# Rotary halves and residual rows added by accumulating DMAs, and new copy durations in a planner

## The chip, the core and the metric

The kernel runs on one core of a Trainium2 chip. A core has TensorE (PE) for matmuls and transposes, VectorE (DVE), ScalarE (ACT) and GpSimd (POOL) for elementwise work, SyncE (SP) whose queue issues the DMAs, 128 partitions of SBUF, and eight PSUM banks of 128 x 512 float32. The metric is the device time of one execution in microseconds (us). Lower is better.

## What is computed

A decoder trunk of two layers in float32 on 1024 tokens of width 1024:

```
x <- x + RMSNorm( W_out [ retention | dilated attention | gated MLP ] ( RMSNorm(x) ) )
x <- x + RMSNorm( W_down ( silu(W_gate h) * W_up h ) ),  h = RMSNorm(x)
```

All mixers read one input projection. Queries and keys of the 6 retention heads and the 6 attention heads (64 wide) get a rotary embedding: `t * cos + rot * sin`, where `rot = concat(-t[32:], t[:32])` swaps the two halves of a head and negates one. The two things the change is about are this sum and the residual sum `x + RMSNorm(f) * g`.

## The kernel before

**Precision by splitting.** Each float32 operand of a large matmul is split into a high part (a rounded copy, tiles `wh`, `hT`, `ph`, `ga`, `wb`) and a low part (source minus high part, `wl`, `pl`), and a product is three matmuls. The copy runs on ACT or DVE, the subtraction on DVE. Banks of 512 columns are evacuated by ACT or DVE.

**Order.** Every helper (`tt`, `stt`, `copy`, `act`, `dma`, `mm`) only records an operation in a `Program`, with its possible engines and a cost in ns for each. Two planners use these costs. While operations are recorded (`Program.add`), a clock per engine estimates when data is ready; generators such as `att_pair`, `ret_pair` and `post_norm` go on when their inputs are ready by that clock, and this sets the order of recording. Then `Program.order` simulates the engines with all operations: whichever is ready with the earliest due time goes next, PE's due times follow the recorded order, and an operation with two engines goes where it would end first. The outcome is the fixed order of instructions on every engine; semaphores make an engine wait where data comes later than planned. For a DMA on SP both planners add 650 ns, the bytes at 360 per ns behind the DMAs before it, and 1000 ns to the issue's cost.

**A rotary half.** A projection of 128 features (two heads) by 1024 tokens is made in two halves of 512 tokens, each a bank `fb` (`feat`). `rope_evac` copies the bank to `z`, has four DMAs of 64 KB copy `z` to `sw` with groups of 32 partitions swapped, and computes `r = z * cos`, `sw = sw * sin`, `r = r + sw`. The sine table carries the sign (`K_SIGN`). There are 24 halves per layer: 12 in the attention part, 12 in the retention part. In attention `r` is read by `att_pair` (copies `ks` of the key) and `att_unit` (copies `qd` of the query), which run as four lanes of softmax work between the projections; in retention by `ret_pair`, whose transposes and score matmuls read `r` directly.

**A residual tile.** `post_norm` is called for each of 8 token tiles after the output projection and after the feed-forward part, in both layers (32 calls). It loads the old row block `xt` (512 KB) early, computes the norm of `f` (ACT square, POOL power in `rms`), multiplies `f` by the gain row, computes `xt = f * ss + xt`, stores `xt`, and, except in the last of the four stages, makes the next norm (`prenorm`, into `nj`) and transposes it on PE (`to_hT`, banks `tb`) into `hT` for the next projection.

POOL runs only the powers of the norms (`ss`, `gn`) and a few memsets; all DMAs are issued on SP.

Of the kernel before, what the change touches and what calls it, by code (L numbers as in the profile page):

```python
# [15 lines left out]
ALU = mybir.AluOpType  # L16
AX = mybir.AxisListType

P = 128
S = 1024  # L20
D = 1024
NT = S // P
NK = D // P
DEPTH = 2
HD = 64
# [11 lines left out]
K_ID, K_TRIL, K_DEC, K_XI, K_ZETA, K_GAM, K_FREQ, K_SIGN, K_END = (  # L37
    0, 128, 256, 1024, 1408, 1414, 1417, 1449, 1577)
# [36 lines left out]
def _constants():  # L75
    c = np.zeros((P, K_END), np.float32)
    i = np.arange(P)
    c[:, K_ID:K_ID + P] = np.eye(P)
    c[:, K_TRIL:K_TRIL + P] = i[:, None] >= i[None, :]
    lg = np.log(1.0 - 2.0 ** (-5.0 - np.arange(6)))  # L80
    diff = (i[None, :] - i[:, None]).astype(np.float64)
    for h in range(6):
        c[:, K_DEC + h * P:K_DEC + (h + 1) * P] = np.where(
            diff >= 0, np.exp(-lg[h] * (i[:, None] + 1.0)) * HD ** -0.5, 0.0)
        c[:, K_ZETA + h] = np.exp(lg[h] * (P - 1.0 - i)) * HD ** -0.5
    for p in range(3):
        for e in range(2):
            rows = slice(e * HD, (e + 1) * HD)
            c[rows, K_XI + p * P:K_XI + (p + 1) * P] = np.exp(lg[2 * p + e] * (i + 1.0))[None]
            c[rows, K_GAM + p] = np.exp(lg[2 * p + e] * P)  # L90
    c[:, K_FREQ:K_FREQ + 32] = (10000.0 ** (-np.arange(0, HD, 2) / HD))[None]
    c[:, K_SIGN:K_SIGN + P] = np.where(i % HD < HD // 2, -1.0, 1.0)[None]

    dist = (NT - 1) * P + i[:, None] - np.arange(S)[None, :]
    count = np.zeros(dist.shape)
    for window, dil in ((128, 1), (512, 4), (2048, 16)):
        count += (dist >= 0) & (dist <= window) & (dist % dil == 0)
    with np.errstate(divide="ignore"):
        mask = np.where(count > 0, HD ** 0.5 * np.log(count), NEG)
    return c, mask.astype(np.float32)  # L100
# [109 lines left out]
class Program:  # L210
# [17 lines left out]
    def add(self, alts, outs, ins, nbytes=0, func=None, **args):  # L228

        op = Op()  # L230
        eng = min(alts, key=lambda e: self.t[e] + alts[e][0])
        cost = alts[eng][0]
        op.alts, op.eng, op.cost, op.args, op.nbytes, op.func = alts, eng, cost, args, nbytes, func
        op.name = outs[0].root.name if outs else ""
        deps = set()
        for r in ins:
            t, (a, b, lo, hi) = r.root, r.box
            for o, w in t.writes:
                if t.psum or (w[0] < b and a < w[1] and w[2] < hi and lo < w[3]):
                    deps.add(o)  # L240
            if t.psum:
                deps.update(o for o, _ in t.reads)
        for r in outs:
            t, (a, b, lo, hi) = r.root, r.box
            hit = False
            for o, w in t.writes:
                if t.psum or (w[0] < b and a < w[1] and w[2] < hi and lo < w[3]):
                    deps.add(o)
                    hit = True
            for o, w in t.reads:  # L250
                if t.psum or (w[0] < b and a < w[1] and w[2] < hi and lo < w[3]):
                    deps.add(o)
            if not hit:
                deps.update(t.before)
        for r in outs:
            t, (a, b, lo, hi) = r.root, r.box
            for x in (t.writes, t.reads):
                x[:] = [(o, w) for o, w in x if t.psum and False or not (
                    a <= w[0] and w[1] <= b and lo <= w[2] and w[3] <= hi) or (t.psum and o.eng != eng)]
            t.writes.append((op, (a, b, lo, hi)))  # L260
        for r in ins:
            r.root.reads.append((op, r.box))
        deps.discard(op)
        op.deps = deps
        self.list.append(op)

        t = self.t[eng]
        for r in ins:
            for k in self.keys(r):
                if r.root.by.get(k) != eng:  # L270
                    t = max(t, r.root.done.get(k, r.root.since))
        for r in outs:
            for k in self.keys(r):
                if r.root.last.get(k) != eng:
                    t = max(t, r.root.used.get(k, r.root.since))
        end = t + cost
        self.t[eng] = end
        if eng == "sp":
            self.t["bw"] = max(self.t["bw"], end + 650) + nbytes / 360
            end = self.t["bw"] + 1000  # L280
        lag = LAT.get((eng, "pe"), 0.0)
        for r in ins:
            for k in self.keys(r):
                if end + lag > r.root.used.get(k, 0.0):
                    r.root.used[k], r.root.last[k] = end + lag, eng
        for r in outs:
            for k in self.keys(r):
                r.root.done[k] = r.root.used[k] = end + lag
                r.root.by[k] = r.root.last[k] = eng

    def order(self):
# [10 lines left out]
                d.users.append(o)  # L302
        for o in reversed(ops):
            if o.eng != "pe":
                cost = o.cost + (o.nbytes / 360 + 1650 if o.eng == "sp" else 0.0)
                o.prio = min((u.prio - LAT.get((o.eng, u.eng), 0.0) * SLACK for u in o.users), default=t) - cost * SLACK
        free = dict(pe=0.0, act=0.0, dve=0.0, pool=0.0, sp=0.0)
        bw, table = 0.0, None
# [23 lines left out]
        while len(done) < len(ops):  # L332
# [38 lines left out]
                table = o.func  # L371
            o.start = best
            o.end = free[eng] = best + o.cost
            if eng == "sp":
                bw = max(bw, o.end + 650) + o.nbytes / 360
                o.end = bw + 1000
            done.append(o)
# [97 lines left out]
def _body(ctx, tc, nc, x, positions, g_mix_pre, g_mix_post, w_in, w_s, b_s, w_out,  # L475
# [36 lines left out]
    def dma(out, in_):  # L512
        outs = [out] if isinstance(out, Ref) else []
        ins = [in_] if isinstance(in_, Ref) else []
        n = 4 * math.prod((outs + ins)[0].shape)
        prog.add(dict(sp=(475.0 if n > 66000 else 650.0, nc.sync.dma_start)), outs, ins, n, out=out, in_=in_)

    in_all = (AF.Copy, AF.Identity, AF.Square)

    def act_cost(o, i, n_ptr=0):  # L520
        return 0.833 * o.size + (51 if i.root.psum else 93) + 93 * n_ptr

    def act(o, i, func=AF.Copy, **kw):
        ptrs = [v for k, v in kw.items() if k != "accum_out" and isinstance(v, Ref)]
# [5 lines left out]
    def copy(o, a, only=None):  # L530

        alts = dict(act=(act_cost(o, a), lambda out, in_: nc.scalar.activation(out=out, in_=in_, func=AF.Copy)),  # L532
                    dve=((1.042 if a.root.psum else 0.521) * o.size + 68, nc.vector.tensor_copy))
        if only:
            alts = {only: alts[only]}
        prog.add(alts, [o], [a], out=o, in_=a)

    def tt(o, a, b, op, on=None):

        alts = {}  # L540
        if on != "pool":
            alts["dve"] = (1.042 * o.size + 68,
                           lambda out, in0, in1: nc.vector.tensor_tensor(out=out, in0=in0, in1=in1, op=op))  # L543
        if on != "dve" and op != ALU.max and not (a.root.psum or b.root.psum):
            alts["pool"] = (300 + 165 * o.size if op == ALU.pow else 150 + 2.11 * o.size,
                            lambda out, in0, in1: nc.gpsimd.tensor_tensor(out=out, in0=in0, in1=in1, op=op))  # L546
        prog.add(alts, [o], [a, b], out=o, in0=a, in1=b)
# [432 lines left out]

    def post_norm(t, f, g_post, g_pre, src, dst, raw=False):

        while U.left < 2:
            yield None
        xt = U.alloc(name="x")
        dma(xt[:], src[t * P:(t + 1) * P, :])
        tmp = U.alloc(name="nj")
        cuts = halves if g_pre is None and t == NT - 1 else whole
        ss = rms(f, tmp, cuts)
        for cs in cuts:  # L990
            tt(f[:, cs], f[:, cs], g_post[:, cs], ALU.mult)
        for cs in cuts:
            stt(xt[:, cs], f[:, cs], ss[:, 0:1], xt[:, cs], ALU.mult, ALU.add)
            dma(dst[t * P:(t + 1) * P, cs], xt[:, cs])
        ST.free(ss)
        U.free(f)
        if g_pre is None:
            hT_done[0] += 1
        else:
            prenorm(xt, g_pre, tmp)  # L1000
            yield from to_hT(tmp, t, raw)
        U.free(xt, tmp)


    def proj_tok(n_units, kper, n, evac, before=None):
# [257 lines left out]


    def rope_evac(r, hf, b):
        z = H.alloc(name="z")
        sw = H.alloc(name="sw")
        copy(z[:], b[:])
        for e in range(4):
            o = e ^ 1  # L1270
            dma(sw[e * 32:e * 32 + 32], z[o * 32:o * 32 + 32])
        cs = slice(hf * 512, hf * 512 + 512)
        tt(r[:, cs], z[:], L["tab"][0][:, cs], ALU.mult)
        tt(sw[:], sw[:], L["tab"][1][:, cs], ALU.mult)
        tt(r[:, cs], r[:, cs], sw[:], ALU.add)
        H.free(z, sw)

    yT = {}
    y_left = {}
# [507 lines left out]
```

## Time and profile before

| | us |
|---|---|
| median of 3 runs (lowest, highest) | 2324.86 (2320.76, 2325.04) |
| the profiled execution | 2320.37 |
| its span, first to last instruction | 2318.6 |

| engine | busy us | share | instructions |
|---|---|---|---|
| PE (matmul) | 2285.3 | 99% | 11320 |
| DVE | 1751.7 | 76% | 3225 |
| ACT | 912.5 | 39% | 1669 |
| POOL | 86.0 | 4% | 95 |

SP's queue moved 223.69 MB. PE's granted clock is full in all 40 slices of the page. A busy share is an average over stages: in the order of the span, layer 1 has the attention projections and the attention (20 to 300 us), retention (300 to 425), output projection and residual (to 535), feed-forward (to 1125) and residual (to 1185); layer 2 repeats this and ends at 2318.6. Matmuls overlap, so a matmul's mean duration is longer than the distance to the next one.

### The profile page before, as it was taken

To read this page: it belongs to the slowest core of one execution; us is meant where nothing else is said; L and a number is where in the kernel's file an instruction comes from. 1 tells how busy PE (TensorE), PEld (TensorE's weight loads), DVE (VectorE), ACT (ScalarE), POOL (GpSimd) and SP (SyncE) were. 2 spreads that over 40 slices of the span, in tenths; PEclk is the share of its full clock that TensorE was granted. 3 is DMA by queue.
4 is the path that set the end of the run, shared out by engine and by line. 5 is a ranking of instruction groups with operands and counts; after the bars stand their busy time and mean duration, and the time that the engine had idled before them with its cause. 6 is when DMAs were issued, how large, how long until landed. Compare 5 with 4: busy or idle time off the path is not lost.

```text
span 2318.6 us, 30306 instructions
## 1 busy us (share of the span) xinstructions
PE 2285.3 (99%) x11320; PEld 1930.7 (83%) x11320; DVE 1751.7 (76%) x3225; ACT 912.5 (39%) x1669; POOL 86.0 (4%) x95
## 2 busy tenths in 40 slices
PE   8999999999999999999999999999999999999998
PEld 7897988888888888878898889888888888888786
DVE  7689676688975554889967978666989755549896
ACT  5368531335122222434334776222541322225341
POOL 0000001010000000000000000010200000000000
PEclk9999999999999999999999999999999999999999
DMA  6211222333432223422342112232523322244142
GB/s 200 68 34 37 65 68 74 105 115 104 132 105 82 83 86 122 179 108 73 127 153 60 33 38 83 61 96 64 179 79 123 101 82 82 82 169 158 55 136 92
DMA packets 213060, 225.63 MB, mean 97 GB/s; under 512 B 14000, under 2 KB 170800, under 8 KB 212912
## 3 DMA queue, kind: packets, MB, share of 16 engines
q1 hardware_dynamic: 212912, 223.69, 30.6%
q8 instruction: 89, 1.46, 0.3%
q14 instruction: 59, 0.48, 0.1%
HBM read 167.01 MB, written 44.04 MB: 91 GB/s over the span
## 4 chain that ended last, share of the span: by engine, by line
PE 82%; DVE 13%; ACT 2%; issue 2%; POOL 1%; DMA 0%; SPq 0%; POOLq 0%; DVEq 0%; ACTq 0%
PE w_b L583 35%; PE db_b L583 17%; PE fb_b L583 15%; PE pb_b L583 6%; DVE f_u L543 3%; PE tb_b L593 2%; DVE x_u L568 1%; PE sb_b L583 1%; PE ob_b L583 1%; PE yb_b L583 1%; DVE pr_u L1760 1%; ACT nj_u L527 1%; PE cb_b L583 1%; DVE pl_h L543 1%; POOL ss_st L546 1%
## 5 line engine op out<-in xcount | busy, mean ns | idle before, releaser
L583 PE MATMUL w_b<-hs_u,wh_u 128*128 128x512 f32 x1280 | 395.0, 389 | 0.0
L583 PE MATMUL db_b<-wb_u,ga_u 128*128 128x512 f32 x1512 | 345.3, 390 | 4.0 <-DVE wb_u L543 3.8
L583 PE MATMUL fb_b<-hT_u,wh_u 128*128 128x512 f32 x1088 | 344.3, 397 | 0.0
L583 PEld LDWEIGHTS db_b<-wb_u,ga_u 128*128 128x128 f32 x1512 | 283.1, 188 | 65.8 <-DVE wb_u L543 5.5
L583 PEld LDWEIGHTS w_b<-hs_u,wh_u 128*128 128x128 f32 x1280 | 239.9, 188 | 51.0 <-ACT wh_u L532 1.5
L583 PE MATMUL w_b<-hT_u,wh_u 128*128 128x512 f32 x832 | 257.1, 390 | 0.0
L583 PE MATMUL w_b<-hs_u,wl_u 128*128 128x512 f32 x640 | 248.7, 389 | 0.0
L583 PEld LDWEIGHTS fb_b<-hT_u,wh_u 128*128 128x128 f32 x1088 | 197.9, 188 | 38.9 <-issue 1.9
L583 PE MATMUL fb_b<-hT_u,wl_u 128*128 128x512 f32 x544 | 213.0, 392 | 0.2
L543 DVE TENSOR_TENSOR c_h<-w_b,c_h 128x512 f32<-128x512 f32 x192 | 131.1, 685 | 81.6 <-PE w_b L583 80.0
L583 PE MATMUL pb_b<-wh_u,hT_u 128*128 128x384 f32 (+1 forms) x768 | 190.5, 323 | 0.1
L543 DVE TENSOR_TENSOR f_u<-f_u,db_b 128x512 f32<-128x512 f32 x232 | 151.3, 678 | 42.7 <-PE db_b L583 42.5
L583 PEld LDWEIGHTS w_b<-hT_u,wh_u 128*128 128x128 f32 x832 | 155.7, 188 | 32.1
L583 PE MATMUL w_b<-hT_u,wl_u 128*128 128x512 f32 x416 | 161.9, 389 | 0.0
L543 DVE TENSOR_TENSOR wl_u<-wr_u,wh_u 128x1024 fp32r<-128x1024 f32 (+1 forms) x130 | 152.4, 1183 | 1.1 <-ACT wh_u L532 0.7
L583 PEld LDWEIGHTS w_b<-hs_u,wl_u 128*128 128x128 f32 x640 | 120.1, 188 | 25.4 <-DVE wl_u L543 0.2
L583 PEld LDWEIGHTS pb_b<-wh_u,hT_u 128*128 128x128 f32 x768 | 135.4, 190 | 1.2 <-DVE wh_u L1760 0.4
L532 ACT ACTIVATE wh_u<-wr_u 128x1024 fp32r<-128x1024 f32 (+1 forms) x93 | 94.7, 1034 | 88.3 <-DVE ws_u L543 50.6
L583 PE MATMUL pb_b<-wl_u,hT_u 128*128 128x384 f32 (+1 forms) x384 | 122.7, 320 | 1.7 <-DVE wl_u L543 1.7
L583 PEld LDWEIGHTS fb_b<-hT_u,wl_u 128*128 128x128 f32 x544 | 102.1, 188 | 23.4 <-DVE wl_u L543 1.0
L532 ACT ACTIVATE c_h<-w_b 128x512 f32<-128x512 f32 x84 | 50.3, 599 | 168.8 <-PE w_b L583 168.8
L543 DVE TENSOR_TENSOR wl_u<-ws_u,wh_u 128x1024 fp32r<-128x1024 f32 x88 | 106.6, 1215 | 0.1
(196 smaller groups left out, 4055.5 us busy)
## 6 DMA issues: line engine op xcount, KB each, us to landing
wr_u<-w_gate_up SPq DMA_DIRECT2D x176, 256.0 KB, 3.8
gs<-c_h SPq DMA_DIRECT2D x88, 256.0 KB, 2.3
wr_u<-gs SPq DMA_DIRECT2D x44, 512.0 KB, 6.7
wr_u<-w_down SPq DMA_DIRECT2D x44, 512.0 KB, 5.5
wr_u<-w_in SPq DMA_DIRECT2D x38, 512.0 KB, 4.4
sw_h<-z_h SPq DMA_DIRECT2D x192, 64.0 KB, 2.0
wr_u<-w_out SPq DMA_DIRECT2D x16, 512.0 KB, 3.9
wr_u<-w_gate_up SPq DMA_DIRECT2D x16, 512.0 KB, 5.8
```

The costliest lines, as they stand in the source:

```text
L527: lambda out, in_, **k: nc.scalar.activation(out=out, in_=in_, func=func, **k))),
L532: alts = dict(act=(act_cost(o, a), lambda out, in_: nc.scalar.activation(out=out, in_=in_, func=AF.Copy)), dve=((1.042 if a.root.psum else ...
L543: lambda out, in0, in1: nc.vector.tensor_tensor(out=out, in0=in0, in1=in1, op=op))
L546: lambda out, in0, in1: nc.gpsimd.tensor_tensor(out=out, in0=in0, in1=in1, op=op))
L568: lambda out, in0, scalar, in1: nc.vector.scalar_tensor_tensor(out=out, in0=in0, scalar=scalar, in1=in1, op0=op0, op1=op1))),
L583: prog.add(dict(pe=(cost + 3, lambda out, lhsT, rhs: nc.tensor.matmul(out, lhsT, rhs, start=start, stop=stop, skip_group_check=on_top))), ...
L593: prog.add(dict(pe=(109.0, lambda out, in_, identity: nc.tensor.transpose(out, in_, identity))), [o], [i, ident], out=o, in_=i, identity=i ...
L1760: op.fn(**{k: v.real() if isinstance(v, Ref) else v for k, v in op.args.items()})
```

## The change

1. `rope_evac` makes no copy. It computes `sw = b * sin` and `r = b * cos` straight from the bank, and four accumulating DMAs of 64 KB on GpSimd's queue add `sw`, with groups of 32 partitions swapped, into `r`. The sign of the sine table is flipped, since the multiplication now comes ahead of the swap.
2. `post_norm` for tiles 0 to 5 computes `f = f * ss * g` in one DVE pass and adds the old rows by an accumulating DMA from DRAM, then stores `f` and goes on with it. Tiles 6 and 7 keep the load, the gain multiply and the addition.
3. A helper `dma_add` records the accumulating DMA on POOL with a cost of 1000 ns; the planners give every operation that moves bytes the DMA's delay, not only those on SP.
4. The planner's fixed costs change: ACT from PSUM 51 to 67 and from SBUF 93 to 190 ns, DVE's copy from SBUF 68 to 155.

```diff
-    c[:, K_SIGN:K_SIGN + P] = np.where(i % HD < HD // 2, -1.0, 1.0)[None]
+    c[:, K_SIGN:K_SIGN + P] = np.where(i % HD < HD // 2, 1.0, -1.0)[None]
...
-        if eng == "sp":
+        if nbytes:
             self.t["bw"] = max(self.t["bw"], end + 650) + nbytes / 360
...
+    def dma_add(out, in_):
+
+        prog.add(dict(pool=(1000.0, lambda out, in_: nc.gpsimd.dma_start(out=out, in_=in_, accum_op=ALU.add))),
+                 [out], [out] + ([in_] if isinstance(in_, Ref) else []), 4 * math.prod(out.shape), out=out, in_=in_)
...
     def act_cost(o, i, n_ptr=0):
-        return 0.833 * o.size + (51 if i.root.psum else 93) + 93 * n_ptr
+        return 0.833 * o.size + (67 if i.root.psum else 190) + 93 * n_ptr
...
-                    dve=((1.042 if a.root.psum else 0.521) * o.size + 68, nc.vector.tensor_copy))
+                    dve=(1.042 * o.size + 68 if a.root.psum else 0.521 * o.size + 155, nc.vector.tensor_copy))
...
-        while U.left < 2:
+        end = t >= NT - 2
+        rs = slice(t * P, (t + 1) * P)
+        while U.left < 1 + end:
             yield None
-        xt = U.alloc(name="x")
-        dma(xt[:], src[t * P:(t + 1) * P, :])
+        if end:
+            xt = U.alloc(name="x")
+            dma(xt[:], src[rs, :])
...
-        for cs in cuts:
-            tt(f[:, cs], f[:, cs], g_post[:, cs], ALU.mult)
-        for cs in cuts:
-            stt(xt[:, cs], f[:, cs], ss[:, 0:1], xt[:, cs], ALU.mult, ALU.add)
-            dma(dst[t * P:(t + 1) * P, cs], xt[:, cs])
+        if end:
+            for cs in cuts:
+                tt(f[:, cs], f[:, cs], g_post[:, cs], ALU.mult)
+            for cs in cuts:
+                stt(f[:, cs], f[:, cs], ss[:, 0:1], xt[:, cs], ALU.mult, ALU.add)
+                dma(dst[rs, cs], f[:, cs])
+        else:
+            stt(f[:], f[:], ss[:, 0:1], g_post[:], ALU.mult, ALU.mult)
+            dma_add(f[:], src[rs, :])
+            dma(dst[rs, :], f[:])
...
-        z = H.alloc(name="z")
         sw = H.alloc(name="sw")
-        copy(z[:], b[:])
+        cs = slice(hf * 512, hf * 512 + 512)
+        tt(sw[:], b[:], L["tab"][1][:, cs], ALU.mult)
+        tt(r[:, cs], b[:], L["tab"][0][:, cs], ALU.mult)
         for e in range(4):
             o = e ^ 1
-            dma(sw[e * 32:e * 32 + 32], z[o * 32:o * 32 + 32])
-        cs = slice(hf * 512, hf * 512 + 512)
-        tt(r[:, cs], z[:], L["tab"][0][:, cs], ALU.mult)
-        tt(sw[:], sw[:], L["tab"][1][:, cs], ALU.mult)
-        tt(r[:, cs], r[:, cs], sw[:], ALU.add)
-        H.free(z, sw)
+            dma_add(r[e * 32:e * 32 + 32, cs], sw[o * 32:o * 32 + 32])
+        H.free(sw)
```

## Rows read from the trace of the kernel before

**Rows 1.** Stages: us, then busy us of PE, PEld, DVE, ACT, POOL.
```profile
0.00:20.00 20.00, 9.76 (x47) 8.15 (x48) 10.14 (x19) 12.28 (x26) 2.05 (x9) 1.00 0.89 310
...
174.00:232.00 58.00, 55.04 (x303) 44.51 (x302) 53.52 (x159) 49.45 (x89) 3.27 (x2) 1.00 0.13 37
...
532.00:535.00 3.00, 2.52 (x18) 2.01 (x17) 2.69 (x4) 3.00 (x6) 0.28 (x1) 1.00 0.93 267
...
1032.00:1040.00 8.00, 6.02 (x24) 3.92 (x23) 8.00 (x15) 6.70 (x13) 0.00 (x0) 1.00 0.00 0
...
1171.00:2308.00 1137.00, 1130.51 (x5584) 954.83 (x5583) 850.97 (x1555) 438.59 (x799) 38.54 (x38) 1.00 0.30 94
2308.00:2318.60 10.60, 0.82 (x4) 0.36 (x2) 5.14 (x10) 0.72 (x2) 1.79 (x2) 0.74 0.26 100
sum 2318.60, PE 2285.26 PEld 1930.74 DVE 1751.66 ACT 912.46 POOL 85.99; mean PE 175.79 PEld 148.52 DVE 134.74 ACT 70.19 POOL 6.61
```

**Rows 2.** What PE waited for: us in total, times, longest us.
```profile
PE db_b L583 <- DVE wb_u L543: 3.8, 4, 1.4
PE ob_b L583 <- DVE pl_h L543: 2.5, 8, 0.5
```

**Rows 3.** Groups: out<-in, shape, count | busy us, mean ns | idle before.
```profile
L543 DVE TENSOR_TENSOR c_h<-w_b,c_h 128x512 f32<-128x512 f32 x192 | 131.1, 685 | 81.6 <-PE w_b L583 80.0 <-issue 0.9
...
L543 DVE TENSOR_TENSOR r_u<-r_u,sw_h 128x512 f32<-128x512 f32 x48 | 33.0, 687 | 0.9
...
L532 ACT ACTIVATE z_h<-fb_b 128x512 f32<-128x512 f32 x46 | 27.5, 598 | 157.5 <-PE fb_b L583 120.7 <-issue 34.3 <-DVE pl_h L543 2.5
```

**Rows 4.** The swaps `sw`: issue ns min/median/max, and landing.
```profile
L1760 SPq DMA_DIRECT2D sw_h<-z_h x192: 507/588/1863, 61.9 to 1554.7; - x192
...
DMA to landing us min/median/max: 1.9/2.0/3.9
```

**Rows 5.** One half in order of time: ACT, then DVE (start us, us, instruction).
```profile
66.69 0.60 ACT L532 ACTIVATE z_h<-fb_b 128x512 f32<-128x512 f32 x1 [4.84 <-PE fb_b L583]
...
72.63 0.69 DVE L543 TENSOR_TENSOR r_u<-r_u,sw_h 128x512 f32<-128x512 f32 x1
73.24 0.28 DVE L1760 CAST qd_h<-r_u 64x256 fp32r<-64x256 f32 x1
```

**Rows 6.** Stages of the first layer's attention.
```profile
55.00:103.00 48.00, 48.00 (x225) 40.10 (x224) 26.78 (x53) 13.18 (x27) 0.00 (x0) 1.00 0.26 72
103.00:142.00 39.00, 38.94 (x235) 34.11 (x234) 34.84 (x93) 26.72 (x57) 0.00 (x0) 1.00 0.23 62
142.00:232.00 90.00, 86.72 (x550) 74.80 (x549) 83.37 (x243) 73.49 (x139) 6.65 (x4) 1.00 0.11 30
```

**Rows 7.** Groups of DVE between 103 and 142 us.
```profile
L543 DVE TENSOR_TENSOR r_u<-r_u,sw_h 128x512 f32<-128x512 f32 x6 | 4.1, 684 | 0.1
```

**Rows 8.** Groups of POOL over the span.
```profile
L546 POOL TENSOR_TENSOR ss_st<-ss_st,nhalf 128x1 f32<-128x1 f32 x64 | 42.9, 674 | 1446.4 <-DVE ss_st L553 1438.7 <-DVE ss_st L568 7.6
...
L546 POOL TENSOR_TENSOR gn_st<-gn_st,nhalf 128x8 f32<-128x8 f32 x20 | 37.2, 1861 | 540.8 <-DVE gn_st L553 540.8
```

**Rows 9.** The gain multiply of the residual part, over the span.
```profile
L543 DVE TENSOR_TENSOR f_u<-f_u,row_u 128x1024 f32<-128x1024 f32 x31 | 37.8, 1219 | 11.0 <-ACT nj_u L527 11.0
```

**Rows 10.** Every transfer of the residual tile `x`, loads and stores.
```profile
DMA to landing us min/median/max: 2.3/4.3/10.0
```

**Rows 11.** DMA issues: count, KB each, median us to landing.
```profile
x_u<-x SPq DMA_DIRECT2D x15, 512.0 KB, 5.8
```

**Rows 12.** One tile's second norm and transposes, in order of time.
```profile
488.19 1.28 DVE L568 SCALAR_TENSOR_TENSOR nj_u<-x_u,ss_st,row_u 128x1024 f32<-128x1024 f32 x1 [0.68 <-POOL ss_st L546]
...
489.53 1.09 PE L593 MATMUL tb_b<-cst,nj_u 128*128 128x128 f32 x8
```

**Rows 13.** Copies from SBUF, over the span.
```profile
L532 ACT ACTIVATE ga_u<-wr_u 128x512 fp32r<-128x512 f32 x76 | 45.9, 622 | 23.5 <-DVE wr_u L543 13.4 <-PE db_b L583 9.8
...
L1760 DVE CAST wh_u<-wr_u 128x1024 fp32r<-128x1024 f32 x34 | 23.3, 686 | 3.3 <-DMA wr_u<-w_in 3.1
```

More of the change, by code (lines that the diff above doesn't have):

```diff
@@ L304, in order @@
             if o.eng != "pe":
-                cost = o.cost + (o.nbytes / 360 + 1650 if o.eng == "sp" else 0.0)
+                cost = o.cost + (o.nbytes / 360 + 1650 if o.nbytes else 0.0)
                 o.prio = min((u.prio - LAT.get((o.eng, u.eng), 0.0) * SLACK for u in o.users), default=t) - cost * SLACK
@@ L373, in order @@
             o.end = free[eng] = best + o.cost
-            if eng == "sp":
+            if o.nbytes:
                 bw = max(bw, o.end + 650) + o.nbytes / 360
@@ L989, in post_norm @@
         ss = rms(f, tmp, cuts)
-        for cs in cuts:
-            tt(f[:, cs], f[:, cs], g_post[:, cs], ALU.mult)
-        for cs in cuts:
-            stt(xt[:, cs], f[:, cs], ss[:, 0:1], xt[:, cs], ALU.mult, ALU.add)
-            dma(dst[t * P:(t + 1) * P, cs], xt[:, cs])
+        if end:
[8 more added lines that the diff above has]
+            dma(dst[rs, :], f[:])
         ST.free(ss)
-        U.free(f)
         if g_pre is None:
@@ L999, in post_norm @@
         else:
-            prenorm(xt, g_pre, tmp)
+            prenorm(f, g_pre, tmp)
             yield from to_hT(tmp, t, raw)
-        U.free(xt, tmp)
+        U.free(f, tmp)
+        if end:
+            U.free(xt)
     def proj_tok(n_units, kper, n, evac, before=None):
```

## The prediction

> **What bounds the kernel now.** The table of stages comes first, since the share of busy time is an average. Its sum line has TensorE (PE) busy for 2285.26 of 2318.60 us, so the idle time of PE is 33.3 us, and nothing that the change does can win more than that unless PE's own work changes, which it doesn't: matmuls and transposes stay the same in number and shape [rows 1]. The reader is to see where the 33.3 us lie: 10.2 us before and among the first matmuls (0 to 20), 9.8 us behind the last ones (2308 to 2318.6), 2.96 us in the first layer's attention (174 to 232), 0.48 us behind its residual rows (532 to 535), 1.98 us in the second product of its feed-forward part (1032 to 1040), 6.5 us in the second layer, which repeats the first, and 1.4 us in small pieces [rows 1]. Without head and tail 13.3 us are left.
>
> Next, who ends PE's waits. In the attention stretch it is the low half of the transposed probabilities, `pl`, written by VectorE (DVE), and in the feed-forward stretch the split weights, also DVE [rows 2]. DVE is busy 34.84 of 39 us between 103 and 142 and 83.37 of 90 between 142 and 232, but only 26.78 of 48 between 55 and 103 [rows 6]. So in the attention stage DVE, not PE, sets the pace from about 103 on; before that it has room.
>
> **The rotary part.** There are 48 halves: two layers, six pairs of heads, query and key, two column halves. Each now costs one copy `z` of 0.60 us on ScalarE (ACT; 46 of 48), four swaps on SP's queue, and three DVE passes of 0.69 us, of which the add stands for all [rows 3]. Afterwards it is two DVE passes, both straight from PSUM, and four accumulating DMAs on POOL's queue. Removed: 48 × 0.687 = 33 us of DVE, 27.5 us of ACT, and 192 SP issues of 0.588 us [rows 3, 4]. A pass with one PSUM operand is not slower: such adds of this shape take 0.685 us [rows 3].
>
> What of this is on the path? Only six of a layer's halves have their last add between 103 and 142, where DVE is full [rows 6, 7]; the six before meet one that is idle for 21 of 48 us, and those of the retention stage meet one with more room still. That is 6 × 0.684 = 4.1 us of DVE per layer, taken out ahead of the holes. PE idles 0.06 + 3.28 us in 103 to 232 [rows 6], less than the 4.1 us, so I let all of it go: 3.3 us per layer, 6.6 in both. What is late next is ACT (73.49 of 90 us there), which also loses 3.6 us of copies.
>
> The latency must not grow. Now a half takes from its copy's start at 66.69 to its last add's end at 72.63 + 0.69 = 73.32, 6.6 us, and its reader (`qd`) starts 0.08 us before that, so there is no slack [rows 5]. Afterwards: two passes 1.38 us, four issues, one landing. No row shows a DMA issued by POOL. An issue lies between SP's shortest (0.507 us) and POOL's longest kind of instruction (1.861 us) [rows 4, 8]; I take 0.674, POOL's instruction on a single column, its nearest row. A landing lies between 1.9 and 3.9 us, the ends of the swaps' own landing; I take their median, 2.0 [rows 4]. Sum: 1.38 + 2.70 + 2.0 = 6.1 us, 0.5 less than now; the ends are 5.3 and 12.7, that is 1.3 less to 6.1 more. I cost it at nothing. The readers (`qd`, `ks` copies) are queued in order on ACT and DVE; behind them stand the bank evacuations and the softmax of other lanes.
>
> A PSUM bank is now held for two DVE passes instead of one ACT copy, 2 × 0.69 - 0.60 = 0.8 us longer. Eight banks and the 24 matmuls of the next half hide it; without that cover it is 48 × 0.8 = 38 us.
>
> **The residual part.** In 24 of 32 calls (tiles 0 to 5) the gain multiply of 1.219 us goes [rows 9], 29 us of DVE in total, in stretches where PE idles at most 0.48 us [rows 1]. I let 0.45 us per layer go, 0.9 in both. The row load moves from SP, where it was issued ahead of need, to POOL behind the tile's own multiply, so its landing joins the chain to the transposes. The planner charges 1.0 + 0.65 + 524288/360 ns + 1.0 = 4.1 us. By rows it is POOL's issue, 0.674 to 1.861 us, and a landing whose median is 4.3 over all transfers of that tile (2.3 to 10.0) and 5.8 for loads of `x` [rows 8, 10, 11]. With 4.3 + 0.67 the landing is 0.9 us later than planned; the ends are 1.1 us earlier and 7.8 us later. PE takes its queue in order, and the first tile's transposes follow `nj` at once: 488.19 + 1.28 = 489.47, then 489.53 [rows 12]. So I charge 0.9 us to the first tile of each of the three stages with transposes, 2.7 us; later tiles follow behind other tiles' matmuls, which hide as much. Without that cover all 18 tiles pay, 16 us. The store of the new row waits for the same landing but nobody waits for it soon.
>
> POOL gains 216 issues, 146 us at 0.674, on top of 86 us [rows 1, 8]. Queued behind a waiting one is the power of the next tile or of the group norm, whose DVE pass waits for it: at most one issue, 0.7 us (1.9), hidden like the bank. Tiles 6 and 7 keep the old form, so the tail stays.
>
> The Trainium skill (DMA: Bandwidth & Descriptors, "Anatomy of one DMA — SWDGE (gpsimd) path") gives a POOL-issued DMA 2.0 us plus its bytes at 436 GB/s; as an estimate 3.2 us for a residual tile, so the 2.7 us would fall away and the sum be 2317.3. The 5.8 us landing of `x` in this trace [rows 11] speaks against it, as it is longer even without an accumulation.
>
> **The cost numbers.** ACT's copy from SBUF of 512 columns takes 622 ns; the planner had 0.833 × 512 + 93 = 520 and gets 616. DVE's cast of 1024 takes 686 ns; it had 601 and gets 688 [rows 13]. No instruction becomes faster; who gets a copy and in which order may change. The bound is one hole of the feed-forward product, 1.98 us per layer, closed or doubled [rows 1]: 4 us either way. There DVE is busy 8.00 of 8 us, so a shift of copies hardly helps: I take 0.
>
> **Sum.** -6.6 - 0.9 + 2.7 = -4.8 us on the profiled execution's own 2320.37 us (1.8 more than its span), so 2315.6. The runs shown have a median of 2324.86, 4.5 above it; against that median the time is 2320.
>
> **Rivals.**
> 1. *No gain.* PE's holes come from one lane's chain (softmax, transpose, `pl`), not from DVE's load, or the planner lets the freed time pass. For it: DVE still idles 10.8 us in 103 to 232 [rows 6]. Against: PE's waits there end on DVE [rows 2]. Then -0.9 + 2.7 = 1.8 us: 2327, with the 4 us of the cost numbers from 2322 to 2331.
> 2. *More gain.* True durations and lighter engines let the planner close every inner hole: 13.3 us, 2312. For it: ACT was planned 16% too short. Against: the feed-forward hole, where the change takes nothing from DVE.
> 3. *Slower by the residual.* At 5.8 + 0.67 us the landing is 2.4 us late. After one stall the following tile is covered by the shift, the next again not, so I count two tiles in each of three stages: 6 × 2.4 = 14.4 us, less 7.5: 2332. It decides from 1.3 us of lateness on. For it: the 5.8 row and the 0.06 us between `nj` and the transposes. Against: the median 4.3, and other tiles' matmuls in between.
> 4. *Slower by POOL's queue.* POOL's issues take 1.7 us. Then a half is 1.38 + 6.8 + 2.0 = 10.2 us long, 3.6 more than now; six readers per layer wait 21.6 us where DVE has 10.8 + 4.1 us free, so PE loses 6.7 per layer: 2338. It decides from 2.5 us of lateness, 1.4 us an issue. For it: POOL's 1.861 us. Against: 0.674, and the free DVE time.
>
> The Trainium skill (SBUF — State Buffer, "SBUF: two separate sides") gives rival 4 a mechanism: a DMA issued from GpSimd needs its descriptors written through ports that DVE holds during a two-port copy. Casts from SBUF run 0.686 us here [rows 13]; an issue that meets one would wait that long by this rule, which would carry 0.674 to 1.36 us. No row shows a POOL DMA, so the trace neither bears it out nor denies it.
>
> **Chances.** Forecast 0.36 (own range 2314 to 2326, by the 4 us of the cost numbers and 2 us of lateness), no gain 0.18, more gain 0.20, residual 0.17, POOL 0.09. What a measurement can tell from no change is 0.2%, 4.6 us. Faster: 0.20 of the forecast, 0.02 of no gain and 0.20 of more gain, 0.42. Slower: 0.01, 0.05 of no gain, 0.14 of residual and 0.08 of POOL, 0.28. Within: 0.30. The range runs from 2305, beyond the rival of more gain by the 4 us of the cost numbers and some planning noise, to 2338, the POOL rival; above it lie the far ends of the unknown landings.
>
> **What would show it.** Right: the stage 103 to 232 with PE idle well under 3.3 us, no DVE wait on `sw`, issues on POOL near 0.7 us, 64 KB landings near 2.0 us, PE waits for the transposes of `nj` under 3 us in all. Wrong: PE waiting on `tb` behind a residual landing for more than 1.3 us a tile (rival 3), POOL issues above 1.4 us with ACT and DVE waiting for `r` (rival 4), or holes unchanged with a lighter DVE (rival 1).

## The result and the profile after

The changed kernel takes 2360.43 us (median of 4 runs, 2358.73 to 2361.06), the kernel before 2324.95 beside it: 1.0156 times as long, 95% interval 1.0143 to 1.0169. It is 35.5 us slower, where 4.8 us less had been forecast.

First the head of the page of the changed kernel: span, then busy us, share and instructions of each engine; the mean granted clock by slices, in tenths.

```profile
span 2359.1 us, 30196 instructions
...
PE 2296.1 (97%) x11320; PEld 1940.4 (82%) x11320; DVE 1707.0 (72%) x3181; ACT 879.5 (37%) x1597; POOL 255.8 (11%) x311
...
PEclk9999999999999999999989999999999999999999
```

DVE and ACT did get lighter, by 44.7 and 33.0 us [rows 1], and PE does the same 11320 matmuls. Yet PE idles 2359.1 - 2296.1 = 63.0 us, not 33.3, and its busy time is 10.8 us longer. One slice of the clock has fallen. So the question is where PE waits. The next two fences cut both kernels at the same times: the first layer's attention and retention (to its first output products), its residual rows, the second residual stage, the second layer's attention and retention, its residual rows. First the kernel after (columns as in [rows 1]).

```profile
20.00:485.00 465.00, 460.24 (x2626) 402.66 (x2627) 337.70 (x824) 198.04 (x395) 101.56 (x115) 1.00 0.29 65
485.00:560.00 75.00, 67.25 (x322) 55.67 (x321) 57.83 (x94) 43.80 (x99) 14.79 (x21) 0.98 0.71 175
...
1100.00:1230.00 130.00, 118.98 (x572) 104.16 (x571) 90.21 (x150) 47.64 (x99) 14.45 (x22) 0.93 0.51 142
1230.00:1640.00 410.00, 406.23 (x2319) 353.93 (x2318) 290.21 (x722) 175.38 (x338) 97.55 (x109) 1.00 0.29 60
1640.00:1760.00 120.00, 113.37 (x524) 93.72 (x523) 91.45 (x132) 53.66 (x113) 15.35 (x22) 0.97 0.45 114
```

The same stretches of the kernel before:

```profile
20.00:485.00 465.00, 461.02 (x2628) 402.76 (x2627) 350.12 (x832) 213.39 (x429) 24.83 (x19) 1.00 0.24 68
485.00:560.00 75.00, 74.52 (x361) 61.98 (x360) 68.82 (x107) 46.30 (x101) 11.66 (x15) 1.00 0.54 169
...
1100.00:1230.00 130.00, 129.60 (x650) 113.24 (x649) 97.72 (x160) 48.72 (x107) 8.73 (x16) 1.00 0.40 130
1230.00:1640.00 410.00, 405.94 (x2317) 351.30 (x2316) 310.36 (x737) 190.15 (x371) 23.07 (x16) 1.00 0.22 64
1640.00:1760.00 120.00, 119.54 (x553) 98.64 (x552) 110.50 (x162) 56.18 (x107) 10.56 (x13) 1.00 0.45 138
```

Two readings. In the stretches of attention and retention (20 to 485 and 1230 to 1640) DVE has lost 12.4 and 20.2 us, and PE is as busy as before, within 0.8 us: the relief bought nothing. In the three residual stretches PE's idle time went from 0.48 + 0.40 + 0.46 to 7.75 + 11.02 + 6.63 us, 24.1 us more, and in the same three the clock fell.

Who is waited for there (waits of the kernel after by engine, line and tile; us in total, times, longest us):

```profile
ACT nj_u L532 <- DMA f_u<-x: 21.8, 6, 6.4
...
ACT nj_u L532 <- DMA f_u<-xb: 20.5, 6, 6.4
...
ACT nj_u L532 <- DMA f_u<-xa: 17.6, 6, 5.6
...
PE w_b L588 <- ACT hT_u L537: 10.9, 2, 5.9
PE pb_b L588 <- DVE wl_u L548: 5.5, 2, 4.4
PE pb_b L588 <- DVE wh_u L1772: 4.8, 1, 4.8
PE tb_b L598 <- DVE nj_u L573: 4.1, 3, 1.8
```

ACT's square of the new row waits for the landing in each of 18 tiles, 59.9 us in all, 3.3 a tile. PE itself waits for `nj`, to transpose it, only 4.1 us, at the first tile of each stage; its long waits name `hT` and weights, tiles that are not late by themselves. The timeline of the last accumulating tile of the first stage shows why (start us, us, instruction, idle before and releaser):

```profile
516.98 1.28 DVE L573 SCALAR_TENSOR_TENSOR f_u<-f_u,ss_st,row_u 128x1024 f32<-128x1024 f32 x1
...
518.90 0.89 POOL L520 DMA_DIRECT2D f_u<-x  x1 [1.95 <-ACT hT_u L537]
...
521.57 1.69 PE L598 MATMUL tb_b<-cst,nj_u 128*128 128x128 f32 x14
...
526.38 1.06 ACT L532 ACTIVATE nj_u<-f_u 128x1024 f32<-128x1024 f32 x1 [6.41 <-DMA f_u<-x]
...
527.56 0.15 DVE L558 TENSOR_SCALAR ss_st<-ss_st 128x1 f32<-128x1 f32 x1 [4.33 <-ACT nj_u L532]
...
528.73 0.37 ACT L537 ACTIVATE hT_u<-tb_b 128x256 fp32r<-128x256 f32 x1
...
529.16 0.79 PE L588 MATMUL w_b<-hT_u,wh_u 128*128 128x512 f32 x1 [5.90 <-ACT hT_u L537]
```

The multiply ends at 518.26, POOL issues at 518.90, the square starts at 526.38: 8.1 us, where the planner had put 4.1. Behind that square stand, in ACT's order, the copies of the *previous* tile's transposes to `hT`, whose matmuls ended at 523.3; PE's next product waits for them, not for the late row. The late landing stops what the planner had queued behind its reader. In the second stage the hole of 4.8 us has the same source, by DVE: the cast of the weights `wh` stands behind the statistics of a square that waits for its row. The hole of 4.4 us there (`wl`, at 1192 us) has not: DVE is at work through it, with the adds of the last two tiles ahead of that split.

After such a hole PE is also slower (second residual stage; the column behind POOL is the granted clock):

```profile
1176.00:1183.00 7.00, 2.19 (x11) 1.75 (x10) 2.60 (x6) 2.19 (x4) 0.75 (x1) 0.83 0.78 184
1183.00:1190.00 7.00, 5.95 (x27) 5.45 (x26) 6.47 (x12) 2.59 (x6) 0.55 (x1) 0.50 1.07 341
1190.00:1200.00 10.00, 5.56 (x25) 5.14 (x23) 9.36 (x16) 6.56 (x16) 1.65 (x3) 0.67 0.92 316
1200.00:1210.00 10.00, 10.00 (x57) 9.50 (x56) 9.44 (x19) 4.96 (x13) 0.00 (x0) 0.95 0.62 151
```

PE idles 4.8 of 7 us, and then works for 7 us at 0.50, its 1.2 GHz level. Busy time times the missing clock, an estimate of what it cost, is 0.4 + 3.0 + 1.8 + 0.5 = 5.7 us for this one stretch.

POOL's side of it (issues: count, KB each, median us to landing), which nothing in the kernel before had shown:

```profile
r_u<-sw_h POOLq DMA_DIRECT2D x192, 64.0 KB, 3.3
...
f_u<-xa POOLq DMA_DIRECT2D x12, 512.0 KB, 6.1
...
f_u<-x POOLq DMA_DIRECT2D x6, 512.0 KB, 6.3
f_u<-xb POOLq DMA_DIRECT2D x6, 512.0 KB, 5.6
```

And one rotary half, which answers to [rows 5]: DVE's two passes, POOL's four issues, the reader.

```profile
61.93 0.69 DVE L548 TENSOR_TENSOR sw_h<-fb_b,tab_u 128x512 f32<-128x512 f32 x1 [1.36 <-PE fb_b L588]
62.54 0.68 DVE L548 TENSOR_TENSOR r_u<-fb_b,tab_u 128x512 f32<-128x512 f32 x1
...
63.88 3.33 POOL L520 DMA_DIRECT2D r_u<-sw_h  x4 [29.20 <-DVE r_u L548]
...
67.51 0.29 DVE L1772 CAST qd_h<-r_u 64x256 fp32r<-64x256 f32 x1 [4.29 <-DMA r_u<-sw_h]
```

The reader takes 64 partitions, so it starts when the first two of the four blocks are in, after 67.51 - 61.93 = 5.6 us. The fourth block's issue and landing (the tile `sw` on POOL from 66.5 to 66.6 us):

```profile
L520 POOL DMA_DIRECT2D r_u<-sw_h x1: 1647/1647/1647, 65.6 to 65.6; - x1
...
DMA to landing us min/median/max: 3.3/3.3/3.3
```

So the half is complete at 68.9, 7.0 us after its first pass began, against 6.6 before and 6.1 predicted. Over all 48 halves the median is 7.9 us, against 6.6 before: the halves became longer.

### The profile page after: what moved, and what is told of

Its sections match the earlier page's. It is cut to its first block, busy times and chain, and to the rows that moved or that the text cites. A ratio compares the mean times of both kernels' runs of the same rounds, so it can differ in the third digit from the quotient of the medians.

```text
span 2359.1 us, 30196 instructions
## 1 busy us (share of the span) xinstructions
PE 2296.1 (97%) x11320; PEld 1940.4 (82%) x11320; DVE 1707.0 (72%) x3181; ACT 879.5 (37%) x1597; POOL 255.8 (11%) x311
## 5 line engine op out<-in xcount | busy, mean ns | idle before, releaser
L520 POOL DMA_DIRECT2D r_u<-sw_h x192 | 156.4, 1238 | 471.7 <-DVE r_u L548 135.4
L551 POOL TENSOR_TENSOR ss_st<-ss_st,nhalf 128x1 f32<-128x1 f32 x64 | 40.7, 641 | 1406.5 <-DVE ss_st L558 1398.9
L532 ACT ACTIVATE nj_u<-f_u 128x1024 f32<-128x1024 f32 (+1 forms) x57 | 59.6, 1045 | 195.9 <-DVE f_u L548 131.5
```

Source lines behind the costliest of these rows:

```text
L520: prog.add(dict(pool=(1000.0, lambda out, in_: nc.gpsimd.dma_start(out=out, in_=in_, accum_op=ALU.add))), [out], [out] + ([in_] if isinsta ...
L532: lambda out, in_, **k: nc.scalar.activation(out=out, in_=in_, func=func, **k))),
```

## The experiments

**The parts apart.** Three kernels take parts of the change alone. The theory at this point (A): the residual part makes the loss, the cost numbers and the rotary part little.

e1, rotary part and cost numbers; all of `post_norm` is as before, of which this line is shown:

```diff
...
-            dma_add(f[:], src[rs, :])
+            stt(xt[:, cs], f[:, cs], ss[:, 0:1], xt[:, cs], ALU.mult, ALU.add)   # xt loaded ahead by SP
...
```

> The rotary part and the new cost numbers alone; the residual rows are added as before. Theory A (the loss comes from the residual adds: PE and ACT take their queues in order and meet a landing some 3 us later than planned): 2319 to 2331 us, PE idle 30 to 38 us in all, no hole above 3 us where the residual tiles are transposed. Rival B (the rotary adds on POOL's queue cost it): above 2345 us.

Measured: 2325.45 us, ratio 1.0007 (0.9998 to 1.0017). As A had it.

e2, the residual part alone (`rope_evac`, the sign row, `act_cost` and `copy` as before).

> The residual part alone, with the old cost numbers and the old rotary part. Theory A: above 2348 us, with PE holes of 4 to 7 us around 520, 1180 and 1690 us and ACT waiting 15 us or more in each of the three stages for the landing of the added rows. Rival B: below 2332 us.

Measured: 2353.21 us, ratio 1.0130 (1.0116 to 1.0144). As A had it; there the wait of PE stands at the transposes (PE's waits, e2):

```profile
PE tb_b L598 <- DVE nj_u L573: 16.1, 7, 6.3
```

e3, the cost numbers alone:

```diff
-        return 0.833 * o.size + (51 if i.root.psum else 93) + 93 * n_ptr
+        return 0.833 * o.size + (67 if i.root.psum else 190) + 93 * n_ptr
-                    dve=((1.042 if a.root.psum else 0.521) * o.size + 68, nc.vector.tensor_copy))
+                    dve=(1.042 * o.size + 68 if a.root.psum else 0.521 * o.size + 155, nc.vector.tensor_copy))
```

> The new copy durations alone. Theory A: within 4 us of before, 2321 to 2329 us, as no instruction gets faster and PE's inner holes are 13 us in all. Rival C (the new numbers bring a worse order, the holes of 1 us each at the start of the feed-forward sums are theirs): above 2331 us.

Measured: 2311.74 us, ratio 0.9951 (0.9938 to 0.9963): 11.3 us faster, a miss for both theories. No work has changed; which engine takes a copy, and the order, have. From its page (e3):

```profile
PE 2279.1 (99%) x11320; PEld 1930.2 (84%) x11320; DVE 1772.2 (77%) x3265; ACT 886.5 (38%) x1625; POOL 83.0 (4%) x95
```

Its profiled span, 2308.9 us, is 9.7 us shorter than before. Only 3.5 of them are idle time of PE; 6.2 are busy time of the same 11320 matmuls, so PE's busy time depends on the order too. The parts are -11.3 (costs), +13.7 (rotary on top of them) and +35 (residual on top of both), each in the one order that its kernel got.

**The residual part.** e4 leaves every instruction of the change and tells the planner that POOL's landings come later, 3.0 us for a row and 0.6 for a rotary block:

```diff
-            end = self.t["bw"] + 1000
+            end = self.t["bw"] + 1000 + (late(nbytes) if eng == "pool" else 0.0)
```

and the same in both places of `order`.

> The whole change, and the planners count 3 us more for a 512 KB add of POOL and 0.6 us more for a 64 KB add, as the trace shows them; nothing else is touched. Theory A as a planning error (a queue that is taken in order meets a landing that the plan put too early): 2320 to 2338 us, the 5 us holes gone. Rival A2 (the load is behind the tile's own result now, and no order hides 7 us per tile): above 2345 us, ACT still waiting over 10 us per stage.

Measured: 2329.76 us, ratio 1.0031 (1.0019 to 1.0043). ACT's waits for the rows fall from 59.9 to 16.3 us (e4):

```profile
ACT nj_u L537 <- DMA f_u<-xa: 7.5, 3, 3.4
ACT nj_u L537 <- DMA f_u<-x: 5.3, 4, 2.3
ACT nj_u L537 <- DMA f_u<-xb: 3.5, 3, 2.3
```

The transfers are the same, and 31 us are gone, as they would be if the landings are not slow for the kernel but later than its order expects. But e4 has another order too, in attention as well, so e12 keeps the order of the change to the letter (PE, ACT, DVE and SP have the same instructions in the same sequence in both traces) and takes the wait away. Each of the 24 POOL DMAs carries the finished row to a scratch instead of adding to it.

```diff
-            dma_add(f[:], src[rs, :])
+            dma_sunk(f[:], src[rs, :])    # same price; dma_start(out=sink[k * P:(k + 1) * P, :], in_=f)
```

> Whole change with its order of instructions kept to the letter, but nobody waits for the residual landing: in place of the accumulation each of the 24 POOL DMAs carries the finished row (same size, same place in POOL's queue) to a scratch that no one reads, so the residual of tiles 0 to 5 is left out of the result. Theory A (the 35 us are the lateness of the landings against the order in which the planner put their readers): 2327 to 2336 us, and the PE holes of 5 us behind nj gone. Theory B (the POOL transfers themselves, or the new order, cost it, by ports, queue or the clock): 2345 us or more.

Measured: 2334.73 us, ratio 1.0052 (1.0035 to 1.0069), as theory A had it: 25.7 us less than the change. The first stretch is as full as before, and most of the 2.3 us that are idle in the third lie at the start of the feed-forward part, where e1 has them too; the middle one keeps one hole of 5.9 us at 1172.0, which ends on a weight split by DVE (e12):

```profile
485.00:560.00 75.00, 74.87 (x363) 62.23 (x362) 63.50 (x100) 46.00 (x103) 12.82 (x21) 1.00 0.58 183
...
1100.00:1230.00 130.00, 124.15 (x615) 109.18 (x614) 88.19 (x148) 44.39 (x99) 18.82 (x30) 0.97 0.42 130
...
1640.00:1760.00 120.00, 117.70 (x547) 96.19 (x546) 102.85 (x150) 58.70 (x117) 13.35 (x22) 1.00 0.45 141
```

So some 25 of the residual part's 35 us are the late landings with what follows from them, holes and clock. The other 9 (2334.73 against e1's 2325.45) are not the landing. That hole is in them. It is the 4.4 us hole of the changed kernel: DVE works without a pause from 1171.9 to the split at 1176.9, on the adds of the last two tiles and copies of `hT` that this order puts ahead of it. Why the planner has them there stays open. The scratch DMA is not quite the same: its issue takes 0.57 us, the accumulating one 0.89.

e6 lets only tiles 0 to 3 accumulate, as a dose:

```diff
-        end = t >= NT - 2
+        end = t >= NT - 4
```

> Whole change, but only the residual rows of tiles 0 to 3 accumulate; tiles 4 to 7 keep the load ahead and the add on DVE. Theory A (the loss is made by the last accumulating tiles, behind which PE has no other matmuls left, and by the clock that falls after their holes): 2325 to 2341 us, and no PE hole over 3 us at the transposes of nj. Theory B (each accumulating tile costs its lateness alike, by the queue in order): the 35 us above the rotary-and-costs kernel (2325.5) shrink to two thirds, 2346 to 2352 us.

Measured: 2339.50 us, ratio 1.0065 (1.0050 to 1.0081). A third of the accumulating tiles gone takes away 21 of 35 us, and the time is in A's range: the last tiles would cost more than their share. But e6 has an order of its own too, so the split between the last tiles and the others (14 us) is not shown.

e7 loads the row behind the multiply by SP and adds on DVE:

```diff
-        while U.left < 1 + end:
+        while U.left < 2:
...
-            dma_add(f[:], src[rs, :])
+            xt = U.alloc(name="x")
+            copy(xt[:, 0:1], f[:, 0:1], "dve")
+            dma(xt[:], src[rs, :])
+            tt(f[:], f[:], xt[:], ALU.add, "dve")
+            U.free(xt)
```

> Whole change, but in tiles 0 to 5 nothing accumulates in the DMA: behind the tile's own multiply a plain load of the row is issued by SP's queue (held back by a one-column copy on DVE), and DVE adds it (1.2 us each). Theory A (the loss comes from a load that is no longer ahead of its use, whatever queue issues it and whoever adds): 2340 us or more, with ACT or DVE waiting some 3 to 6 us a tile for the x rows. Theory B (POOL's queue or the accumulation is what is slow; a plain load from SP would land as the planner says): 2332 us or less.

Measured: 2347.22 us, ratio 1.0101 (1.0087 to 1.0114). The time is A's, its sign is not: DVE waits for these loads only 3.8 us in all (e7), and they land about when the planner says, 3.8 us from the start of the issue: in 3.1 to 3.8 us between 482 and 515, 1134 and 1160, and 1652 and 1683 us, where `x` has no other transfers.

```profile
DVE f_u L548 <- DMA x_u<-xa: 2.8, 3, 2.0
...
DVE f_u L573 <- DMA x_u<-xa: 0.7, 1, 0.7
DVE f_u L548 <- DMA x_u<-x: 0.3, 1, 0.3
```

Most of this kernel's loss must then sit elsewhere: in the longer chain, in the 24 adds that are back on DVE, or in the order; no run parts these. It says nothing against POOL's landing being the late one, and does not tell the load behind the multiply from the accumulation as A and B were meant to.

**The rotary part.** Why does it cost 13.7 us on top of the cost numbers?

e5, the rotary part alone, with the old cost numbers and residual rows.

> Rotary part alone: residual rows and cost numbers as before. Theory A (the attention holes come from one lane's chain of softmax, transpose and low half, not from DVE's load, so taking 33 us off DVE buys nothing): 2319 to 2331 us, the DVE busy sum about 25 us or more below before, PE idle in the first layer's 142 to 232 us still over 2.5 us. Theory B (the rotary part costs time by itself, since its POOL adds come late: the 13.7 us by which it spoils the cost numbers' gain are its own): 2332 to 2342 us. Theory C (the prediction's own step, relief closes the holes): under 2319 us.

Measured: 2334.82 us, ratio 1.0048 (1.0035 to 1.0062). In this order the prediction's own step (C) is out, and the time is B's. In e13 nobody waits for the adds, with the order of e1 to the letter:

```diff
-            dma_add(r[e * 32:e * 32 + 32, cs], sw[o * 32:o * 32 + 32])
+            dma_sunk(r[e * 32:e * 32 + 32, cs], sw[o * 32:o * 32 + 32])    # the block goes to a scratch
```

> Rotary part and new cost numbers, residual rows as before (2325.45 us), its order kept to the letter, but nobody waits for the rotary adds: each of the 192 POOL DMAs carries its block of sw to a scratch, so the rotated half is left out of the result. Theory A (the adds land late for their readers, which is what the 13.7 us are): 2310 to 2317 us. Theory B (they land in time; it is the order of the softmax lanes that the other prices led to): 2320 to 2329 us, with the holes of PE at 184 and 223 us where they were.

Measured: 2324.97 us, ratio 1.0006 (0.9997 to 1.0016), against 2325.45 with the waits. In e1's order the adds are not late for anyone who matters. B of e5 named late adds as the cause; e5's own order was not run this way, so there it is not shown. The stretch with the holes is the same in e1 (first) and e13:

```profile
190.00:232.00 42.00, 40.03 (x219) 31.94 (x218) 38.52 (x110) 36.89 (x68) 4.07 (x2) 1.00 0.12 32
```

```profile
190.00:232.00 42.00, 40.03 (x217) 31.91 (x217) 38.43 (x111) 37.20 (x68) 4.12 (x2) 1.00 0.13 32
```

So the landings are not it; the order is left, or what the instructions themselves cost. e9, e14 and e15 have the instructions of e1 and differ in what the planner is told of POOL's rotary adds alone (in `add`, and likewise in `order`):

```diff
-            end = self.t["bw"] + 1000                                    # e1; issue 1000
+            end = self.t["bw"] + (200 if eng == "pool" else 1000)        # e9; issue 800
+            end = self.t["bw"] + (400 if eng == "pool" else 1000)        # e14; issue 800. e15: issue 700
```

> Rotary part and new cost numbers, residual rows as before (2325.45 us as it was), with the planner told what the trace shows of the rotary adds: 800 ns an issue on POOL instead of 1000, and the landing 0.8 us earlier (measured 4.3 us from the second pass to the reader, planned 5.8). Theory A (the rotary part loses because the planner takes its halves for longer than they are): 2306 to 2318 us. Theory B (its halves were never late or early enough to matter; the loss is one of the order in which the softmax lanes fall, which the price does not mend): 2319 to 2333 us, with holes of PE before ob and tb in the second half of attention again.

> The kernel with the fitted prices for POOL's rotary adds (2341.8 us) with one number changed: the landing is put 0.4 instead of 0.2 us behind the last issue. Every instruction is the same, and 0.2 us is within what the landings scatter. Theory A (the order is a lottery, so that a small change of a price moves the attention stage by many us): far from 2341.8, at 2310 to 2326 us, with the holes of 200 to 250 us gone or elsewhere. Theory B (the price itself matters: truer landings of POOL make it worse by a mechanism): 2334 to 2345 us.

> Rotary part and new cost numbers, residual rows as before, the landing 0.4 us behind the last issue as in the run of 2321.95 us, and POOL's issue at 700 ns in the planner instead of 800. Theory A (the rotary part is worth nothing by itself, and a lucky order with it comes as far as the cost numbers alone, 2311.7): 2308 to 2316 us. Theory B (the 33 us that it takes off DVE do close holes once the order is good): 2305 us or less. Theory C (with the POOL adds no order gets there): 2319 us or more.

Measured: e9 2341.79 us (1.0082, 1.0066 to 1.0097), slower than either theory had it; e14 2321.95 (0.9991, 0.9981 to 1.0000), as A had it; e15 2317.56 (0.9971, 0.9960 to 0.9983), between its A and C. A price 0.2 us apart, with the same instructions, moves the kernel by 19.8 us. Late adds do not part the two: from 100 to 240 us the engines wait 2.0 us for one in e9, 2.3 us in e14.

Whether truer prices help can't be read from these three. e9's expectation took 4.3 us, the wait of a reader of two blocks, for a whole half. In the half shown above the second block lands 4.2 us and the fourth 5.7 us behind the second pass, which ends at 63.2. e1's prices put these at 3.8 and 5.8 us (two or four issues of 1.0, then 0.65, 0.18 for the bytes, and 1.0), e9's at 2.6 and 4.2: the old prices were the truer ones. In one stretch, e9, e14, e15 and e3, in this order:

```profile
190.00:232.00 42.00, 37.15 (x222) 30.88 (x220) 33.74 (x117) 28.57 (x56) 0.00 (x0) 1.00 0.10 26
```

```profile
190.00:232.00 42.00, 42.00 (x242) 35.77 (x242) 35.97 (x90) 32.44 (x57) 3.54 (x2) 1.00 0.17 45
```

```profile
190.00:232.00 42.00, 41.72 (x242) 35.39 (x241) 39.91 (x110) 30.29 (x52) 6.69 (x4) 1.00 0.11 29
```

```profile
190.00:232.00 42.00, 42.00 (x269) 38.35 (x267) 39.15 (x119) 30.16 (x58) 0.00 (x0) 1.00 0.17 51
```

PE idles 4.9 us where DVE has 8.3 us free, not at all where DVE has 6.0, and 0.3 and 0.0 us where DVE has 2.1 and 2.9: DVE's load does not decide. That it is which lanes' matmuls are left to cover a softmax is a reading that no run isolates.

e10 swaps by SP and adds on DVE:

```diff
...
-            dma_add(r[e * 32:e * 32 + 32, cs], sw[o * 32:o * 32 + 32])
+            dma(z[e * 32:e * 32 + 32], sw[o * 32:o * 32 + 32])
+        tt(r[:, cs], r[:, cs], z[:], ALU.add)
```

> Rotary part and new cost numbers, residual rows as before, but POOL takes no part: the two passes read PSUM as in the change, SP swaps the product into another tile, and DVE adds it, so DVE gets its third pass back (33 us) and only ACT's 48 copies are gone. Theory A (POOL's accumulating DMAs are what loses the 13.7 us): 2308 to 2318 us, like the cost numbers alone. Theory B (it is the reading straight from PSUM, which takes a copy from ACT that was hidden and puts two passes on DVE before the bank is free, or the new order): 2320 us or more.

Measured: 2315.27 us, ratio 0.9966 (0.9952 to 0.9979). The time is A's, but in e1's order e13 rules out the wait for POOL's adds, and e15 with POOL comes within 2.3 us of it. It may be no more than one more order.

**The cost numbers.** e8 makes half of their correction, e11 twice of it (`act_cost` +142 and +287 from SBUF, DVE's copy 112 and 242).

> Before, with only half of the correction to the planner's copy durations (ACT from SBUF +142 instead of 93 or 190, from PSUM 59; DVE from SBUF 112 instead of 68 or 155). No instruction gets another duration. Theory A (truer numbers give a better order, gain by gain): between the two, 2313 to 2320 us. Theory B (the order is a lottery: any other number reorders attention, and the 11.3 us were one draw): anywhere, most likely outside, 2321 to 2332 us, with holes at other places than in either.

> Before, with the correction of the planner's copy durations made twice as large as the change makes it (ACT from SBUF +287, from PSUM 83; DVE from SBUF 242). Half of it gave 2320.9 us, all of it 2311.7, none 2323 to 2325. Theory A (truer numbers give a better order): worse than the true ones, 2316 us or more. Theory B (a planner that shies from copies on ACT and DVE's SBUF casts does better whatever the truth): 2311 us or less.

Measured: e8 2320.91 us (0.9989, 0.9980 to 0.9998), between the ranges of its two theories; e11 2318.20 (0.9978, 0.9968 to 0.9987), as A had it. None, half, all and double give 2323, 2320.9, 2311.7 and 2318.2: the true numbers are best, but with orders that scatter by 24 us under the rotary part (2317.6 to 2341.8), four draws don't show that truth is the reason. e3, the cost numbers alone, is the fastest kernel of this study and beats both.

## Why the prediction was wrong

**What bounds the kernel.** The list of PE's idle time was right. The limit that it was to set on a gain took PE's busy time as fixed, and e3 shows 6.2 us less of it for the same matmuls. Reading "PE's waits end on `pl`, written by DVE" as "DVE's load sets the pace" was wrong.

**The rotary part, -6.6 us forecast.** The half was to become 0.5 us shorter and became 0.4 us longer in the one shown (7.0 for 6.1 forecast): four issues take 3.33 us for 2.70, the first starts 0.66 us behind the second pass, which the sum didn't have, and the last block lands 1.7 us behind the last issue's end for 2.0. That this costs nothing came true in e1's order (e13), though not because the half is shorter. The relief was real: DVE 12.4 and 20.2 us lighter in the two stretches of attention and retention. The step that failed is "less than the 4.1 us, so I let all of it go": PE's busy time there didn't move. Rival 1's sign, holes unchanged with a lighter DVE, came; e9 and e14 against e15 and e3 show that DVE's load doesn't decide, and that one lane's chain does is argued. What the rotary part costs by itself can't be told from the scatter of orders; the best of its kernels (2317.6) stays above the cost numbers alone.

**The residual part, +1.8 net forecast.** This is the step that decided. Two things in it failed. The lateness was sized at 0.9 us, from an issue of 0.67 and a landing of 4.3, a median over loads and stores; measured are 0.3 to 0.64 us from the multiply to the issue and medians of 5.6 to 6.3 from there to the landing, so 2.0 to 2.7 us late at the medians and 4.0 in the tile shown. The term charged with it, 2.7 us for the first tiles, came out at 4.1, PE's waits for `nj`. (The Trainium skill, DMA: Bandwidth & Descriptors, "Anatomy of one DMA — SWDGE (gpsimd) path", from which 3.2 us were estimated for a row, is below all of these medians: the measurement decides.) And "later tiles follow behind other tiles' matmuls, which hide as much" counted PE's queue alone. The wait stands on ACT, in all 18 tiles, and ACT's and DVE's queues run in order too: the previous tile's `hT` copies and the next weights stood behind the waiting square. Late in a stage that reached PE as holes of 5 to 6 us, so "all 18 tiles pay, 16 us" wasn't the upper end that it seemed; at the measured lateness it would be 36 to 49 us, so other matmuls did hide a part, though not nearly all. The clock, which had no term, added to it, by the estimate 5.7 us in the stretch shown. Rival 3 had the lateness, 2.4 us, but counted it at PE's own transposes, 14.4 us for some 25; it didn't have the way over ACT's and DVE's queues.

**POOL's queue.** Rival 4 didn't come: the four issues of a rotary half take 3.33 us, 0.83 each, and a row's 0.89, and e13 shows that in e1's order nobody on the path waits for `r`.

**The cost numbers, 0 (4 either way) forecast.** Measured -11.3. The bound was taken from one hole of the feed-forward product; the gain came ahead of that, in attention and retention, where a price moves the order of every lane: the first layer's output projection begins at 410.7 us in e3, at 416.5 before. "No instruction becomes faster" is true and proves nothing about the time.

**The sum.** Forecast -6.6 - 0.9 + 2.7 + 0; measured, one part on top of another, -11.3 (costs), +13.7 (rotary), +35 (residual).

## What to carry to other kernels

A transfer moved from ahead of its need to behind a computation costs time wherever it lands later than the order was planned with: 2 to 3 us in each of 18 tiles made some 25 us here. Don't price its landing by a median over loads and stores, and look at what stands behind its reader on *that reader's* engine. If a planner writes the order, price a new kind of DMA from a run before trusting it, and measure how far a change of price alone moves the time: here 20 us for 0.2, more than any gain looked for. A busy engine that ends the waits need not be the bound: see first whether PE's time follows that engine's load from one order to another. And read a reader's wait by what the reader needs: one that takes two of four blocks says nothing of the fourth.

## What the runs showed of the hardware

- An accumulating row DMA from POOL (512 KB) lands 5.6 to 6.3 us after its issue at the median, longer than the 4.3 that the sum had used. For the first four or five tiles of the three stages with transposes it is 5.3 to 6.7 us; in e7, where SP loads the row at the same place without accumulating, 3.1 to 3.8.
- POOL's issue for an accumulating DMA is recorded with 0.89 us for a row; four in a row for 64 KB blocks take 3.33 us, 0.83 each. A plain one of a row to a scratch in DRAM takes 0.57 (e12).
- After 4.8 us of idling within 7, PE ran at a granted 0.50 for 7 us, at 0.67 in the next ten, in which it idled 4.4 us, and at 0.95 in the ten from 1200 on.
- The same 11320 matmuls kept PE busy for 2285.3 us before and 2279.1 in e3, at a mean granted clock of 0.999 in both.
